# A hybrid decoder layer on one core: the first k group in seven products, LayerNorm's moments shifted, other orders for the pointwise and output products

## The chip, the core and the metric

The kernel runs on one core of a Trainium2 chip. Its time is the device time of one execution in microseconds (us); "the median" is that of several executions. A profiled execution also gives a trace: every instruction of each engine with its start and its duration. The engines are TensorE (PE, matrix products), VectorE (DVE), ScalarE (ACT), GpSimd (POOL) and SyncE (SP, which here only starts transfers). POOL too starts transfers, among them accumulating ones, which add their source to their destination.

## What is computed

The input x has 512 tokens of 2048 channels. The reference, cut to what matters:

```python
h = rms_norm(x, norm_g)
z = h @ w_in                                    # 2048 -> 7 x 1024
a_val, a_glu, a_gate, q, k, v, b_gate = split(z)
u = a_val * sigmoid(a_glu)                      # mixer A
u = causal_depthwise_conv(u, conv_w, conv_b)    # 31 taps
u = silu(layer_norm(u, conv_norm_g, conv_norm_b))
u = u @ conv_pw_w + conv_pw_b                   # 1024 -> 1024, "pointwise"
y_a = u * silu(a_gate)
q, k = rms_norm(q per head), rms_norm(k per head)   # mixer B, 16 heads of 64
o = dilated_attention_mixture(q, k, v)          # three windows
y_b = o * silu(b_gate)
out = x + concat(y_a, y_b) @ w_out              # 2048 -> 2048
```

## The kernel before

All large products are made channel by token, 128 channels by 512 tokens at a time, in PSUM tiles `ps_l`. Each f32 operand is split into a high and a low f16 part, and a product is three matmuls: high by high, high by low, low by high (`tri`, lines 414 to 416). Weights come in tiles `wf` of 4 x 128 rows by 512 columns (1 MB), through a ring of eight. For each tile ACT makes the high part (`split_hi`, `wh`) and DVE the low part (`split_lo`, `wl`), with a scale that is worked out from the sum of squares of the group's weights (`measure`, `bound`; each bound ends in a small sum on PE, a few steps on POOL, and `ws` and `wi` on DVE). Only the first two groups are made exactly, with f32 operands, line 895.

A **group** is 512 output columns of one part of `w_in` (`vg` value and GLU gate, `q`, `k`, `v`, `ag` and `bg` the two gates), of the pointwise weights (`pw`) or of `w_out` (`wb` and `wa`); a **unit** is one weight tile of it. The list `GROUPS` sets the order of units. A unit has eight **slots**: in each, PE makes six matmuls of 512 columns, and the other engines' work is written between the slots. Three mechanisms decide what is written where:

- `after(n, fn)` puts `fn` into a calendar n slots ahead, and `plan` lists do the same for the units in products of the kind below.
- `run_conv` writes a piece of the convolution (`cv`, DVE) whenever the DVE work written so far is behind a pace (`PACE`, ns per slot); LayerNorm is the tail of the same generator, `conv`.
- The engines run their own queues in order, each as soon as its waits are over. So an instruction that waits holds back everything behind it on its engine.

Groups in `SEVEN` are made with **seven products** instead of eight: the 2048 rows, the 512 columns and the tokens are halved, sums of weight blocks (`s1` to `s4`) and of x blocks (`tx`, from `xs`) are made, and 28 slots of twelve matmuls of 256 columns take the place of 32 slots. Their weights' sums are partly added by POOL's accumulating transfers (`wf<-wf`). The four output groups `wa` are always made so (`seven_parts`, `seven_products`), over `LENGTH` slots each. `w_out` has 16 row blocks, of 128 rows: rows 0 to 7 multiply mixer A's result y_a and 8 to 15 mixer B's, y_b, whose halves `b0` and `b1` have bounds of their own or share the one of y_a. `JOINED` names the output groups in which rows 8 to 11 (`b0`) are part of the seven products, with weights `wsd`; elsewhere they are plain units, `wb`.

LayerNorm before (lines 565 to 609): DVE adds the eight `cv` tiles into `lnacc`, PE sums over the channels (line 576), ACT makes `mean`, DVE subtracts it from each tile, ACT squares, DVE adds the squares into `lnacc2`, and `token_rsqrt` (line 391) sums these on PE with four small f32 products (line 395). Then each tile is scaled, passed through SiLU and split into `u16` for the pointwise product, which evacuates with a `tensor_scalar` and a multiplication by the gate.

Of the kernel before, what the change touches and what calls it, by code (L numbers as in the profile page):

```python
# [10 lines left out]
F32 = mybir.dt.float32  # L11
# [8 lines left out]
P = 128  # L20
S = 512
# [18 lines left out]
PACE = 1230  # L40
# [18 lines left out]
PACE_2 = 1480  # L59
MEASURE = 12  # L60
# [26 lines left out]
def layer(ctx: ExitStack, tc: tile.TileContext, xt, w1, w2, w3, g_in, conv_w, conv_b,  # L87
# [106 lines left out]
    def bound(name, sums, done, top=TOP):  # L194
# [7 lines left out]
        def sum_up():  # L202
            ps = s_ps.tile([P, S], F32, name="ps_s")
            T.matmul(ps[:, 0:n], ones16, sums, start=True, stop=True)
            V.tensor_reduce(scale, ps[:, 0:n], axis=AX.X, op=OP.add)
            G.tensor_scalar(scale, scale, 1e-30, 2.0 ** (-2 * top), op0=OP.max, op1=OP.mult)  # L206
            rsqrt(scale)
# [6 lines left out]
        after(2, sum_up)  # L214
        after(4, finish)
# [28 lines left out]
    for kind, g in GROUPS:  # L244
        if kind == "pw":
            units += [(w2, g, p, kind, g) for p in range(8 // KU)]
        elif kind in OUT_K:
            units += [(w3, g, p, kind, g) for p in OUT_K[kind] + (2,) * (kind == "wa" and g in JOINED)]
# [20 lines left out]
    def measure(i):  # L269
        if n_exact <= i < len(units):  # L270
            group = units[i][3:]
            mine = of_group[group]
# [6 lines left out]
            if not to_measure[group]:  # L279
                after(4, lambda: bound("w", sums.pop(group), lambda s, v: wscale.update({group: (s, v)}),  # L280
# [25 lines left out]
    def split_lo(i):  # L306
        if i < n_plain:
# [3 lines left out]
            after(11 if of_next(i) in SEVEN else 9, lambda: measure(i + RING))  # L311
# [79 lines left out]
    def token_rsqrt(acc, n, eps, c, row):  # L391

        pt = s_ps.tile([P, S], F32, name="ps_s")
        for t in range(NT):
            T.matmul(pt[:, 2 * t:2 * t + 2], acc[:, t * P:(t + 1) * P], ones[:, 0:2], start=True, stop=True)
        V.tensor_scalar(c, pt[:, 0:2 * NT].rearrange("p (t two) -> p t two", two=2)[:, :, 0], 1.0 / n, eps,
                        op0=OP.mult, op1=OP.add)
        rsqrt(c)
        yield
# [5 lines left out]
        yield  # L405
# [16 lines left out]
    def evac_scale(group):  # L422

        if group not in escale:
            other = {"pw": "u", "wa": "yab", "wb": "yb0"}.get(group[0])
# [83 lines left out]
    def evac_qk(half_i, t, ps, is_k):  # L509
# [9 lines left out]
        n = [2, 6 + 4 * t, 7 + 4 * t, 9 + 4 * t]  # L519
        if is_k and ("v", half_i) in SEVEN:  # L520
            n = [4 + 5 * (t > 0), 10 + 2 * t + 2 * (t > 0), 11 + 2 * t + 2 * (t > 0), 13 + 2 * t + 2 * (t > 0)]
# [22 lines left out]

    def conv():

        for i0 in range(0, 8, 2):
# [16 lines left out]
            elif i0 < 6:  # L564
                for i in (i0, i0 + 1):
                    V.tensor_add(acc, acc, cv[i])
                    yield 0

        wait[1] = True
        for i in (6, 7):  # L570
            V.tensor_add(acc, acc, cv[i])
        yield 3
        while any(0 <= clock[0] - n < 8 for n in at_pair.values()):
            yield 1
        mean = s_ps.tile([P, S], F32, name="ps_s")
        T.matmul(mean, ones, acc, start=True, stop=True)
        yield 1
        mean_sb = temp("mean")
        A.activation(mean_sb, mean, AF.Copy, scale=1.0 / C)
        acc = None  # L580
        yield 2
        acc2 = slot("lnacc2")
        squares = []
        for i in range(8):
            V.tensor_sub(cv[i], cv[i], mean_sb)
            if len(squares) > 1:
                V.tensor_add(acc2, acc2, squares.pop(0))
            if i == 0:
                A.activation(acc2, cv[i], AF.Square)
            else:  # L590
                squares.append(temp("lnsq"))
                A.activation(squares[-1], cv[i], AF.Square)
            yield 1 + i % 2
        while squares:
            yield 1
            V.tensor_add(acc2, acc2, squares.pop(0))
        yield 4
# [3 lines left out]
        row = temp("lnrow")  # L601
# [887 lines left out]
```

## Time and profile before

| what | value |
|---|---|
| median of 3 executions | 812.6 us (812.58 to 812.92) |
| the profiled execution | 812.95 us, span of its instructions 811.2 us |
| PE busy | 805.5 us (99%) |
| DVE busy | 707.2 us (87%) |
| ACT busy | 561.3 us (69%) |
| POOL busy | 136.2 us (17%) |
| PE's granted clock | full throughout |

In the rows quoted below, a row of a timeline has the start, the duration, the engine, the line and operation, the output and inputs by the program's names, the shape, and in brackets how long the engine was idle before and what it waited for. DVE's operations all have line 82 (a helper), so they are told apart by their tiles. Durations of instructions that follow each other closely overlap; the distance between two starts is what one costs. A row of windows has the stretch, its length, the busy time with the number of instructions, PE's clock, the share of the transfer engines and their GB/s. A row of transfers has the number, the size of each and the median time from issue to landing.

### The profile page before, as it was taken

How to read it: one execution, taken by the hardware profiler on the slowest of the kernel's cores; microseconds unless marked ns; L12 is line 12 of the kernel's file. 1: busy time of each engine (PE TensorE's matmuls, PEld its weight loads, DVE VectorE, ACT ScalarE, POOL GpSimd, SP SyncE). 2: the span in 40 equal slices, each digit the busy share in tenths (PEclk: the TensorE clock that was granted, in tenths of full speed). 3: DMA queues.
4: the chain of work that ended last, by engine and by line, in shares of the span. 5: the costliest groups of instructions: out<-in, count | busy, mean ns of one | idle time of the engine just before them, and what ended most of it. 6: DMA issues, size and time to landing. Idle time of an engine off the chain costs nothing.

```text
span 811.2 us, 13603 instructions
## 1 busy us (share of the span) xinstructions
PE 805.5 (99%) x5341; PEld 508.8 (63%) x5341; DVE 707.2 (87%) x1188; ACT 561.3 (69%) x788; POOL 136.2 (17%) x147
## 2 busy tenths in 40 slices
PE   9999999999999999999999999999999999999998
PEld 6888745888646854444444444444444447888887
DVE  6668999878989979999999989996689799979885
ACT  6667687577756688586756747587699968965541
POOL 0001021322223400004012010000100003432420
PEclk9999999999999999999999999999999999999999
DMA  9952345983875882526573634426352397898752
GB/s 337 355 212 91 117 93 144 136 255 57 308 150 108 121 296 94 128 104 169 143 182 102 164 112 125 118 88 165 104 120 102 110 278 165 170 249 198 131 103 68
DMA packets 100000, 127.19 MB, mean 157 GB/s; under 512 B 62560, under 2 KB 85344, under 8 KB 90720
## 3 DMA queue, kind: packets, MB, share of 16 engines
q1 hardware_dynamic: 80544, 107.37, 42.2%
q0 software_dynamic: 19104, 18.88, 16.3%
q8 instruction: 41, 0.67, 0.3%
q14 instruction: 23, 0.19, 0.1%
q10 hardware_dynamic: 288, 0.07, 0.0%
HBM read 88.56 MB, written 4.19 MB: 114 GB/s over the span
## 4 chain that ended last, share of the span: by engine, by line
PE 92%; DVE 4%; ACT 2%; DMA 1%; issue 1%; POOL 0%; ACTq 0%; DVEq 0%
PE ps_l L414 24%; PE ps_l L415 24%; PE ps_l L416 24%; PE ps_l L895 10%; PE ps_s L415 2%; PE ps_s L414 2%; PE ps_s L416 2%; PE ps_o L782 2%; PE ps_s L741 2%; DVE ws L82 1%; DMA pt<-hl 1%; DVE wl L82 1%; ACT junk L192 0%; DMA wf<-w_dram 0%; DVE cv L82 0%
## 5 line engine op out<-in xcount | busy, mean ns | idle before, releaser
L82 DVE SCALAR_TENSOR_TENSOR cv<-u,cw,cv 128x511 f32<-128x511 f32 (+14 forms) x240 | 162.0, 728 | 0.4 <-ACT cv L552 0.4
L192 ACT ACTIVATE junk<-wf 128x2048 uint8<-128x2048 f32 x68 | 129.2, 1900 | 9.4 <-DMA wf<-w_dram 9.0
L414 PE MATMUL ps_l<-x,wh 128*128 128x512 f16 x320 | 121.3, 379 | 0.4 <-DVE glu L82 0.4
L416 PE MATMUL ps_l<-x,wl 128*128 128x512 f16 x320 | 121.3, 379 | 0.0
L415 PE MATMUL ps_l<-x,wh 128*128 128x512 f16 x320 | 121.3, 379 | 0.0
L301 ACT ACTIVATE wh<-wf,ws 128x2048 f16<-128x2048 f32 x42 | 83.7, 1994 | 52.0 <-PE ps_l L415 50.2
L82 DVE SCALAR_TENSOR_TENSOR wl<-wf,ws,wh 128x2048 f16<-128x2048 f32 x43 | 100.9, 2346 | 12.1 <-ACT wh L301 12.1
L414 PE MATMUL ps_l<-wh,x 128*128 128x512 f16 x256 | 97.1, 379 | 0.0
L416 PE MATMUL ps_l<-wh,x 128*128 128x512 f16 x256 | 97.0, 379 | 0.0
L415 PE MATMUL ps_l<-wl,x 128*128 128x512 f16 x256 | 97.0, 379 | 0.0
L82 DVE SCALAR_TENSOR_TENSOR ws<-wf,ws 128x1024 f16<-128x1024 f32 x70 | 89.2, 1279 | 7.0 <-ACT ws L1173 4.5
L414 PEld LDWEIGHTS <-wh 128*128 128x128 f16 x448 | 43.9, 98 | 51.5 <-issue 4.0
L416 PEld LDWEIGHTS <-wl 128*128 128x128 f16 x448 | 43.8, 98 | 50.0 <-DVE wl L82 0.4
L415 PEld LDWEIGHTS <-wh 128*128 128x128 f16 x448 | 43.8, 98 | 47.1 <-issue 0.8
L895 PE MATMUL ps_l<-xr,wr 128*128 128x512 f32 x288 | 69.9, 398 | 0.1
L895 PEld LDWEIGHTS ps_l<-xr,wr 128*128 128x128 f32 x288 | 54.5, 190 | 13.7 <-ACT xr L339 1.0
L206 POOL TENSOR_SCALAR ws<-ws 128x1 f32<-128x1 f32 x20 | 9.4, 470 | 306.9 <-DVE ws L82 259.8
L414 PEld LDWEIGHTS <-x 128*128 128x128 f16 x352 | 34.4, 98 | 32.5 <-issue 1.9
L416 PEld LDWEIGHTS <-x 128*128 128x128 f16 x352 | 34.4, 98 | 31.3
L415 PEld LDWEIGHTS <-x 128*128 128x128 f16 x352 | 34.4, 98 | 30.1
L1173 ACT ACTIVATE ws<-wf,ws 128x1024 f16<-128x1024 f32 x42 | 47.1, 1138 | 5.7 <-PE ps_l L416 4.8
L170 POOL TENSOR_TENSOR ss<-ss,half 128x8 f32<-128x8 f32 x16 | 31.5, 1970 | 116.4 <-DVE ss L82 116.3
(265 smaller groups left out, 1871.3 us busy)
## 6 DMA issues: line engine op xcount, KB each, us to landing
wf<-w_dram SPq DMA_DIRECT2D x72, 1024.0 KB, 5.2
wf<-wf POOLq DMA_DIRECT2D x30, 512.0 KB, 6.3
x<-xt_dram SPq DMA_DIRECT2D x16, 256.0 KB, 6.6
res<-xt_dram SPq DMA_DIRECT2D x8, 512.0 KB, 6.7
out_dram<-res SPq DMA_DIRECT2D x15, 256.0 KB, 3.8
wf<-w_dram SPq DMA_DIRECT2D x7, 512.0 KB, 7.2
wf<-wf POOLq DMA_DIRECT2D x12, 256.0 KB, 5.8
wf<-w_dram SPq DMA_DIRECT2D x2, 256.0 KB, 3.4
```

Of the source, the lines that this page charges most:

```text
L82: return getattr(self.engine, name)(out, src, *args, **kw)
L170: G.tensor_tensor(ap, ap, half.to_broadcast(list(ap.shape)), op=OP.pow)
L192: A.activation(junk[:, :n], src, AF.Square, scale=scale, accum_out=acc)
L206: G.tensor_scalar(scale, scale, 1e-30, 2.0 ** (-2 * top), op0=OP.max, op1=OP.mult)
L301: A.activation(parts[i][0], raw[i], AF.Copy, scale=wscale[units[i][3:]][0])
L414: T.matmul(ps, ah, bh, start=first, stop=False, skip_group_check=more)
L415: T.matmul(ps, ah, bl, start=False, stop=False, skip_group_check=more)
L416: T.matmul(ps, al, bh, start=False, stop=last, skip_group_check=more)
L741: T.matmul(ps[i, a], qk["q", hf][p4 // 2][rows, p4 % 2, q, i * P:w], qk["k", hf][p4 // 2][rows, p4 % 2, k, :w], start=n == 0, stop=n == 2)
L782: T.matmul(po[rows, i * P:(i + 1) * P], vs[hf][j // 2][:, j % 2, 2 * p4 + a, vp * DH:(vp + 1) * DH], got["t", a][:, pp * (ALL // P) + FROM ...
L895: T.matmul(banks[group, m], wt[:, a, m * P:(m + 1) * P], xk[b], start=k == 0 and a == b == 0, stop=k == KC - 1 and a == 1)
L1173: A.activation(t[:, 0], block(name, pair), AF.Copy, scale=wscale[group][0])
```

## The change

1. The first k group joins `SEVEN`, with tables (`IN_ADD`, `IN_HI`, `IN_OUT`, `NORM_7`) for the slots of its steps, and the x sums run from slot 60 in steps of 9 (before 58 and 10).
2. LayerNorm: after six tiles PE sums them, and ACT makes the mean of these six as a shift (`shifted`). It is subtracted from all tiles, and six are squared while the convolution of the last pair runs. Five of the additions of squares, and two of the additions of `cv`, are accumulating transfers of POOL. The last two tiles are squared when the convolution ends; their sum `lnlast` (that of all tiles is nil but for these two, after the shift) gives the rest of the mean, and the variance is the mean of squares less its square (`less` in `token_rsqrt`).
3. The order of groups: `pw` comes one unit later (behind `wb` 0), both `pw` groups share one scale, and the evacuation is one operation, with the bias scaled ahead (`pw_bias`).
4. `JOINED` becomes (1, 2): output group 0 has rows 8 to 11 (`wb` 0) and rows 12 to 15 (a new unit `wc`) as plain units, its seven products take 14 slots, and `b1` gets a bound and scale of its own.
5. Slots: the low half of a weight one slot later (`SPLIT_AT`), `measure` and `bound` at other slots, a pace of seven steps instead of two, and tables for the `wa` groups (`WA_PARTS`, `WA_ADD`, `WA_OUT`).

```diff
-PACE = 1230
+PACE_FROM = (65, 117, 171, 227, 299, 363)
+PACE = [1170, 1350, 1300, 1295, 1480, 1465, 1480]
...
-          ("ag", 0), ("ag", 1), ("bg", 1), ("pw", 0), ("pw", 1)]
-JOINED = (0, 1)
-GROUPS += [("wb", g) for g in range(4) if g not in JOINED] + [("wa", g) for g in range(4)]
-OUT_K = {"wb": (2,), "wa": (3, 0, 1)}
-
-SEVEN = (("vg", 3), ("q", 0), ("v", 0))
+          ("ag", 0), ("ag", 1), ("bg", 1), ("wb", 0), ("pw", 0), ("pw", 1), ("wb", 3), ("wc", 0)]
+JOINED = (1, 2)
+GROUPS += [("wa", g) for g in range(4)]
+OUT_K = {"wb": (2,), "wc": (3,), "wa": (3, 0, 1)}
+
+SEVEN = (("vg", 3), ("q", 0), ("k", 0), ("v", 0))
-SUM_FROM = 58
-SUM_STEP = 10
+SUM_FROM = 60
+SUM_STEP = 9
+SPLIT_AT = [0, 3]
...
 def token_rsqrt(acc, n, eps, c, row, less=None):
...
+            for n_sum, a in enumerate((acc,) if less is None else (acc, less)):
+                at = 2 * (NT * n_sum + t)
+                T.matmul(pt[:, at:at + 2], a[:, t * P:(t + 1) * P], ones[:, 0:2], start=True, stop=True)
...
+    def square(i):
+        V.tensor_sub(cv[i], cv[i], shift[0])
+        if not acc2:
+            acc2.append(temp("lnacc2"))
+            A.activation(acc2[0], cv[i], AF.Square)
+        else:
+            squares.append(temp("lnsq"))
+            A.activation(squares[-1], cv[i], AF.Square)
+
+    def shifted():
+        ps = s_ps.tile([P, S], F32, name="ps_s")
+        T.matmul(ps, ones, shift[0], start=True, stop=True)
+        A.activation(shift[0], ps, AF.Copy, scale=1.0 / (6 * P))
+        yield
+        for i in range(6):
+            square(i)
+            yield
+            if squares:
+                yield
+                nc.gpsimd.dma_start(acc2[0], squares.pop(0), accum_op=OP.add)
...
         for i in (6, 7):
-            V.tensor_add(acc, acc, cv[i])
...
+            square(i)
+        last2 = temp("lnlast")
+        V.tensor_add(last2, cv[6], cv[7])
+        yield LN_STEPS[1]
+        for _ in range(2):
+            V.tensor_add(acc2[0], acc2[0], squares.pop(0))
...
+        mean_ps = s_ps.tile([P, S], F32, name="ps_s")
+        T.matmul(mean_ps, ones, last2, start=True, stop=True)
...
         elif kind == "pw":
-            t = temp("ya")
-            V.tensor_scalar(t, ps, evac_scale(group), pwb[:, i:i + 1], op0=OP.mult, op1=OP.add)
             y = ag.pop(i)
-            def gate():
-                V.tensor_mul(y, y, t)
-                put_y("a", i, y)
-            after(1, gate)
+            V.scalar_tensor_tensor(y, ps, pwb[:, i:i + 1], y, op0=OP.add, op1=OP.mult)
+            put_y("a", i, y)
...
-    LENGTH = [29, 28, 21, 21]
+    LENGTH = [14, 28, 28, 21]
...
-            adds = [(-8, "s3", add), (-2, "s2", add), (3, "s1", add), (4, "s4", add),
...
-            begin = {"a11": -6, "a11d": -4, "a22": -3, "a22d": 4, "a12": 0, "s1": 6, "a12d": 11, "s3": 12, "s1d": 14, "s2": 15,
-                     "s3d": 18, "s4": 20, "s2d": 21, "s4d": 24}
+WA_ADD = [{'s1': (4,), 's4': (1,), 's2': (-2,), 's3': (-8,)}, ...
+WA_PARTS = [{'a11': (-29,), 'a22': (-27,), 'a12': (-1,), 's3': (1,), 's2': (4,), 's1': (7,), 's4': (9,)}, ...
...
-                extra[0].append(lambda: split_hi(i + 1))
-                extra[2].append(lambda: split_lo(i + 1))
+                extra[SPLIT_AT[0]].append(lambda: split_hi(i + 1))
+                extra[SPLIT_AT[1]].append(lambda: split_lo(i + 1))
```

In the two `WA` rows (shown for output group 0) the numbers are slots from the group's start: `WA_ADD` says when a sum of weights is formed, `WA_PARTS` when ACT makes its high part; DVE makes the low part one slot later. Before, `adds` and `begin` said the same.

The order of instructions shows where three of these land. First DVE in the third `vg` group, between the evacuation of a first product (`u`, `glu`) and the low half `wl` of the second unit's weights. `xn` is a normalised x tile, `x_…` its low part. Before:

```order
L82 SCALAR_TENSOR_TENSOR xn<-x,gs,rrow 128x512
L82 TENSOR_TENSOR xs<-xn 128x256 x2
L82 SCALAR_TENSOR_TENSOR xs<-xs,xn 128x256 x2
L82 TENSOR_TENSOR glu<-ps_l,rrow 128x512
L82 TENSOR_TENSOR u<-ps_l,rrow 128x512
L82 TENSOR_TENSOR u<-u,glu 128x512
L82 TENSOR_TENSOR x_940<-xn,x_940 128x512
L82 SCALAR_TENSOR_TENSOR xn<-x,gs,rrow 128x512
L82 TENSOR_TENSOR tx<-xs,tx 128x2x256 x2
L82 TENSOR_TENSOR x_967<-xn,x_967 128x512
L82 SCALAR_TENSOR_TENSOR wl<-wf,ws,wh 128x2048
```

The same place in the changed kernel:

```order
L103 SCALAR_TENSOR_TENSOR xn<-x,gs,rrow 128x512
L103 TENSOR_TENSOR glu<-ps_l,rrow 128x512
L103 TENSOR_TENSOR u<-ps_l,rrow 128x512
L103 TENSOR_TENSOR u<-u,glu 128x512
L103 TENSOR_TENSOR xs<-xn 128x256 x2
L103 SCALAR_TENSOR_TENSOR xs<-xs,xn 128x256 x2
L103 TENSOR_TENSOR x_936<-xn,x_936 128x512
L103 SCALAR_TENSOR_TENSOR xn<-x,gs,rrow 128x512
L103 TENSOR_TENSOR x_967<-xn,x_967 128x512
L103 TENSOR_TENSOR tx<-xs,tx 128x2x256 x2
L103 SCALAR_TENSOR_TENSOR xn<-x,gs,rrow 128x512
L103 SCALAR_TENSOR_TENSOR wl<-wf,ws,wh 128x2048
```

The four `xs` operations stand behind the second `glu` instead of ahead of it, and one `xn` more stands ahead of `wl`.

Second, the end of the convolution: DVE before, from the last `cv` subtractions on,

```order
L82 TENSOR_TENSOR cv<-cv,mean 128x512
L82 TENSOR_TENSOR lnacc_5516<-lnacc_5516,lnsq 128x512
L82 TENSOR_REDUCE ws<-ps_s 128x1
L82 ISA sx,st_5720<-ps_s,tab 128x512
L82 ISA st_5720 128x1
L82 ISA sx,st_5721<-ps_s,tab 128x512
L82 ISA st_5721 128x1
L82 SCALAR_TENSOR_TENSOR wl<-wf,ws,wh 128x2048
```

and in the changed kernel DVE, where `sx` is the evacuation of attention scores,

```order
L103 SCALAR_TENSOR_TENSOR cv<-u,cw,cv 128x482
L103 TENSOR_TENSOR cv<-cv,lnacc 128x512 x3
L103 TENSOR_TENSOR lnlast<-cv 128x512
L103 ISA sx,st_5902<-ps_s,tab 128x512
L103 ISA st_5902 128x1
L103 ISA sx,st_5903<-ps_s,tab 128x512
L103 ISA st_5903 128x1
L103 TENSOR_TENSOR lnacc_5241<-lnacc_5241,lnsq 128x512 x2
L103 SCALAR_TENSOR_TENSOR wl<-wf,ws,wh 128x2048
```

and POOL, up to its part of LayerNorm's reciprocal root (`lncol`):

```order
L601 DMA lnacc_5241<-lnsq 128x512
L227 TENSOR_SCALAR ws<-ws 128x1
L191 TENSOR_TENSOR ws<-ws,half 128x1
L227 TENSOR_SCALAR ws<-ws 128x1
L191 TENSOR_TENSOR ws<-ws,half 128x1
L601 DMA lnacc_5241<-lnsq 128x512 x2
L459 TENSOR_TENSOR esc<-wi,xinv 128x1
L601 DMA lnacc_5241<-lnsq 128x512 x2
L227 TENSOR_SCALAR ws<-ws 128x1
L191 TENSOR_TENSOR ws<-ws,half 128x1
L191 TENSOR_TENSOR lncol<-lncol,half 128x4
```

The additions of squares between the subtractions are gone from DVE, `lnlast` is new, and five transfers stand in POOL's queue; `lnlast` waits for the last of them, since it takes its source's buffer.

Third, POOL at the output groups, before,

```order
L427 TENSOR_TENSOR esc<-wi,yabi 128x1
L1026 TENSOR_SCALAR nesc<-esc 128x1
L1030 TENSOR_TENSOR wjs<-ws,yabs 128x1
L1031 TENSOR_TENSOR wjs<-wjs,yb0i 128x1
L955 DMA wf<-wf 128x4x256
L955 DMA wf<-wf 128x2x256
L955 DMA wf<-wf 128x4x256
```

and in the changed kernel:

```order
L459 TENSOR_TENSOR esc<-wi,yb1i 128x1
L1034 DMA wf<-wf 128x4x256 x4
L1034 DMA wf<-wf 128x2x256 x2
L459 TENSOR_TENSOR esc<-wi,yabi 128x1
L1085 TENSOR_SCALAR nesc<-esc 128x1
L1089 TENSOR_TENSOR wjs<-ws,yabs 128x1
L1090 TENSOR_TENSOR wjs<-wjs,yb1i 128x1
```

Six additions for groups 0 and 1 stand together ahead of the scales of the next group.

More of the change, by code (lines that the diff above doesn't have):

```diff
@@ L567, in conv @@
                     yield 0
+            if i0 == 4:
+                shift.append(acc)
+                steps = shifted()
+                for n in range(40):
+                    after(SHIFT_FROM + n * SHIFT_STEP, lambda: next(steps, None))
         wait[1] = True
+        yield LN_STEPS[0]
+        for _ in steps:
+            pass
         for i in (6, 7):
-            V.tensor_add(acc, acc, cv[i])
[L572 to L597, printed above, removed]
+            square(i)
[4 more added lines that the diff above has]
+            V.tensor_add(acc2[0], acc2[0], squares.pop(0))
+        yield LN_STEPS[2]
         while any(0 <= clock[0] - n < 8 for n in at_pair.values()):
@@ L869, in run_conv @@
     def run_conv():
[L871 removed]
+        pace = PACE[sum(clock[0] >= n for n in PACE_FROM)]
         V.load = min(max(V.load - pace, -pace), 4 * pace)
```

317 lines of the change are left out of this document (170 added, 147 removed).

## The prediction

> **What bounds the kernel now.** I read the page first: busy times, then the chain that ended last. After them came the list of what TensorE (PE) waits for, then single rows of PE and VectorE (DVE) at the places the change touches. PE is busy in 805.5 of 811.2 us and carries 92% of the chain; DVE is next with 87%, so it has some 100 us of air, but not everywhere.
>
> ```profile
> span 811.2 us, 13603 instructions
> PE 805.5 (99%) x5341; PEld 508.8 (63%) x5341; DVE 707.2 (87%) x1188; ACT 561.3 (69%) x788; POOL 136.2 (17%) x147
> PE 92%; DVE 4%; ACT 2%; DMA 1%; issue 1%; POOL 0%; ACTq 0%; DVEq 0%
> PE ps_l L414 <- DVE glu L82: 0.4, 1, 0.4
> PE ps_s L741 <- DVE st L82: 0.3, 1, 0.3
> PE ps_l L415 <- DVE ws L82: 0.2, 1, 0.2
> PE ps_o L782 <- DMA pt<-hl: 0.2, 1, 0.2
> ```
>
> In the last four rows the columns are total, times and longest wait: after the start, PE hardly waits. So the time is PE's content plus very little. A gain must come out of PE's content, and every new lateness of DVE or of a transfer that exceeds its slack is paid in full.
>
> **PE's content, step by step.** A matmul's own duration (0.38 us) overlaps the next one, so the price is the distance between starts.
>
> ```profile
> 171.89 0.27 PE L414 MATMUL ps_l<-x,ws 128*128 128x256 f16 x1
> ...
> 172.98 0.27 PE L415 MATMUL ps_l<-x,ws 128*128 128x256 f16 x1
> 542.77 1.02 PE L576 MATMUL ps_s<-lnacc,ones 128*128 128x512 f32 x2
> 543.63 0.38 PE L414 MATMUL ps_l<-x,wh 128*128 128x512 f16 x1
> ...
> 544.28 0.38 PE L414 MATMUL ps_l<-x,wh 128*128 128x512 f16 x1
> 578.61 0.95 PE L395 MATMUL ps_s<-ones,lnacc 128*128 128x2 f32 x8
> 579.42 0.38 PE L414 MATMUL ps_l<-x,wh 128*128 128x512 f16 x1
> ```
>
> Ten starts lie between the first two rows: 0.109 us for 256 columns. Three lie between 543.63 and 544.28: 0.217 us for 512. The f32 column sum (L576, one matmul in the program) holds PE for 0.86 us, and the four small f32 products of the LayerNorm column (L395, x8 in the trace) for 0.81 us.
>
> - First k group in seven products: 192 matmuls of 512 columns (four units of eight slots of six) become 336 of 256 (28 slots of twelve): 41.7 becomes 36.6, −5.1 us.
> - Rows 12 to 15 plain for output group 0, and `JOINED` moved from groups 0 and 1 to 1 and 2: 48 matmuls of 512 come, 96 of 256 go: +10.4 − 10.5, −0.1 us.
> - LayerNorm: a second f32 column sum (one for the shift, one for the mean of what is left), +0.86. `token_rsqrt` now also takes `lnlast`: four more small products, +0.81.
> - One more bound (`yb1`): one small sum on PE, about a tenth of the 0.81, +0.1.
>
> Sum: −3.4 us. Nothing hides this term, because PE is the bound; if no wait grew, the run would end near 812.6 − 3.4 = 809.2 us.
>
> **Place A, the first f16 units (86 to 122 us).** The sums `xs` and `tx` for the seven products start two slots later (`SUM_FROM` 58 to 60), and the low half of a weight (`split_lo`) is asked for one slot later.
>
> ```profile
> 96.42 0.40 PE L895 MATMUL ps_l<-xr,wr 128*128 128x512 f32 x1
> 97.20 0.38 PE L414 MATMUL ps_l<-x,wh 128*128 128x512 f16 x1 [0.38 <-DVE glu L82]
> 107.77 0.38 PE L415 MATMUL ps_l<-x,wh 128*128 128x512 f16 x1
> 108.10 0.39 PE L416 MATMUL ps_l<-x,wl 128*128 128x512 f16 x1
> 86.52:108.04 21.52, 21.18 (x33) 1.00 0.29 98
> 103.23 0.74 DVE L82 SCALAR_TENSOR_TENSOR xn<-x,gs,rrow 128x512 f32<-128x512 f32 x1
> 103.90 1.29 DVE L82 TENSOR_TENSOR tx<-xs,tx 128x512 f16<-128x512 f32 x2
> ...
> 105.70 2.34 DVE L82 SCALAR_TENSOR_TENSOR wl<-wf,ws,wh 128x2048 f16<-128x2048 f32 x1
> ...
> 116.99 0.15 DVE L82 TENSOR_SCALAR ws<-ws 128x1 int32<-128x1 int32 x1
> 117.17 0.16 DVE L82 RECIPROCAL wi<-ws 128x1 f32<-128x1 f32 x1
> ```
>
> DVE is busy in 21.18 of 21.52 us here (the window row: length, busy, instructions), and PE waits for it twice: about 0.5 us for `glu`, and 0.12 us for the second `wl` (108.10 comes 0.33 after 107.77, not 0.22). DVE is the bound of this place, so what is put ahead of that `wl` is paid. The order of the changed kernel has one `xn` more ahead of it (0.67 us between starts), and the pair `ws`, `wi` of a scale (0.15 to 0.25). That is +0.8 to +0.9 us; I take +0.9. The ends are 0 (the pair and the `xn` find a gap) and 1.5 (the third `wl`, which also gets work ahead of it, runs out of its slack).
>
> **Place D, the end of the convolution (about 551 to 567 us).** Before, all sums of LayerNorm were additions on DVE. Now five squares go through accumulating DMAs issued by GpSimd (POOL) into `lnacc2`, each waiting for the one before. The addition `lnlast` on DVE reuses the buffer of the last square, so it waits for the last DMA to land. Queued behind it on DVE stand two score evacuations, two `lnacc` additions and a `wl`.
>
> ```profile
> wf<-wf POOLq DMA_DIRECT2D x12, 256.0 KB, 5.8
> 567.12 0.69 DVE L82 CUSTOM_DVE_ANT_0 sx<-ps_s,tab 128x512 f32<-128x512 f32 x1 [3.67 <-PE ps_s L741]
> 568.35 2.35 DVE L82 SCALAR_TENSOR_TENSOR wl<-wf,ws,wh 128x2048 f16<-128x2048 f32 x1
> 570.61 0.69 DVE L82 TENSOR_TENSOR lnacc<-lnacc,lnsq 128x512 f32<-128x512 f32 x1
> DMA  9999979999994999400000000000000000948997
> ```
>
> Counting the program's work slot by slot, the fifth square is ready near 555 us: ACT does it behind a `gate` evacuation that waits for PE. With 5.8 us to land (the nearest row: the same kind and size) `lnlast` starts near 561. Then come 0.6 + 2 × 0.6 + 2 × 0.6 + 2.26 = 5.3 us, so `wl` is done near 566.3, and PE wants it near 566.5. It just fits or just fails; the second batch of scores also needs the banks that the first two `sx` free, near 563. The DMA engines are idle in the middle of this stretch (the last row shows 550 to 575 us in 40 slices), which favours a landing that isn't slower than 5.8. I take +0.3, ends 0 and 2.
>
> Here the Trainium skill speaks, in "DMA: Bandwidth & Descriptors" (section on the anatomy of one SWDGE DMA): such a DMA takes about 2.0 us plus its bytes over 436 GB/s, which by an estimate from that formula is 2.6 us for 256 KB. By it D would cost nothing and the sum would be 0.3 us lower. The trace's 5.8 disagrees, and I go by the trace.
>
> **Place C, output groups (672 to 710 us).** `wa0` now lasts 14 slots instead of 29. A seven slot is 12 × 0.109 = 1.31 us.
>
> ```profile
> 680.00:700.00 20.00, 19.69 (x33) 1.00 0.56 86
> 690.00:710.00 20.00, 20.00 (x30) 1.00 0.82 171
> wf<-wf POOLq DMA_DIRECT2D x3, 512.0 KB, 5.7
> wf<-wf POOLq DMA_DIRECT2D x3, 256.0 KB, 14.6
> wf<-wf POOLq DMA_DIRECT2D x1, 512.0 KB, 12.3
> ```
>
> The two windows show DVE full before the change, with PE not waiting. The DMA rows are those issued in 669 to 690 us (the first) and in 696 to 702 (the other two). The sums of weights that POOL adds by DMA used to have 20, 17 and 16 slots from the addition to the first use by ACT; the new tables give `s3` 9, `s2` 6 and `s4` 8, the shortest being 7.9 us. Against the 5.7 of the nearest place that holds; against the 12.3 of four in a row it doesn't. DVE has the splits of `wa0` and `wa1` closer together, and `y<-gate,yb1s` for `wc0` ahead of them, which by my count is about 0.15 us late. I take +0.5 for both; ends 0 and 5.
>
> **Stalls that go.**
>
> ```profile
> 625.54 0.38 PE L414 MATMUL ps_l<-u,wh 128*128 128x512 f16 x1
> 625.97 0.38 PE L415 MATMUL ps_l<-u,wh 128*128 128x512 f16 x1
> ```
>
> The pointwise product now starts behind a `wb` unit, 8 × 1.3 = 10.4 us later against LayerNorm, so this wait for `u` (0.43 − 0.22 = 0.21) should go: −0.2. Its cover is that unit; if LayerNorm ends over 10 us later than before, the wait is back. The other moves I cost at nothing: the seven products of k put about 33 us of DVE work beside 36.6 us of PE. `pw`'s evacuation loses a step on DVE and gains none on PE. The accumulating DMAs of `lnacc` have a whole convolution pair to land.
>
> **Sum.** −3.4 + 0.9 + 0.3 + 0.5 − 0.2 = −1.9 us. The profiled run took 812.95 us (span 811.2 and 1.75 around it), so this makes 811.05; the median, 812.6, is 0.35 lower, so 810.7 us. Least: −3.4 and all four named waits gone (0.5 + 0.12 + 0.2 + 0.2), 808.2. Most: +1.5 + 2 + 5 − 3.4, 817.7.
>
> **Rivals.** About 0.2% (1.6 us) is what a measurement can tell from no change: faster is below 811.0, slower above 814.2.
>
> 1. The saving comes whole: A finds a gap, D and C fit their slack. 812.6 − 3.4 − 0.2 = 809.0; with half of A, 809.5. For it: PE waits nowhere else before. Against: DVE's 21.18 of 21.52.
> 2. DVE eats it: A 1.5, D 1.5, C 1.0, also 0.3 at the start of k's products, as before at `ws` (0.2 in the list). 812.6 − 3.4 + 4.3 − 0.2 = 813.3; with half of the extras about 812. For it: the full windows. Against: k's products have slack by count.
> 3. Slower: the landing of `s2` in `wa0`. ACT waits for it from 7.9 us after its issue; the product needs it ten slots after the issue, 13.1 us, less 1.1 for ACT's half and 1.2 for DVE's, so 10.8. Landing in 14.6, as in the last group of rows, would hold PE for 3.8 us: 810.7 + 3.8 = 814.5. It decides from a landing of 14.3 us on. Against: only one stretch of the trace shows such landings, where four were issued together.
>
> A rule of the Trainium skill bears on rival 3: "SBUF — State Buffer", section "Who interferes with whom", says that POOL, while DVE runs a copy or a tensor_scalar in a two-port mode, can't write the descriptors of its DMAs. No row here separates this from a plain queue behind other transfers.
>
> **Chances.** Forecast (810.0 to 811.5) 0.40, rival 1 (809.9 or less) 0.24, rival 2 (811.6 to 814) 0.25, rival 3 0.11. Faster: rival 1 and about two thirds of the forecast, 0.52; same 0.36; slower 0.12. The range reaches from rival 1 to the top of rival 2: 808.9 to 813.8.
>
> **What the changed profile would show.** PE: 336 matmuls of 256 columns where k had 192 of 512, 28 slots in 36.6 us. A: `glu` wait near 0.6, the gap ahead of the first product with the second `wl` near 0.8 instead of 0.12. D: DVE idle for 5 to 8 us ahead of `lnlast`, put down to a DMA, and PE's wait behind it under 1 us. C: DVE's windows at 20 of 20, PE's waits for `ws` or `wsd` under 1 us together, no wait of ACT for a POOL DMA over 2 us. 626: no gap. The prediction is wrong if PE's waits together exceed 3.5 us, or if A's gaps are gone.

## The result, and the profile after

The changed kernel takes 832.1 us (median of six executions, 827.6 to 834.8) against 812.7 for the one before on the same chip: ratio 1.023, 95% interval 1.020 to 1.026. The prediction said 810.7 with a range of 808.9 to 813.8, so it was wrong in sign and by 21 us. The profiled execution took 830.74 us, 17.8 more than the 812.95 of before. First the page of the changed kernel: span, busy times, PE's granted clock in 40 slices, and the chain that ended last by engine.

```profile
span 829.0 us, 13900 instructions
PE 807.0 (97%) x5448; PEld 520.1 (63%) x5448; DVE 716.6 (86%) x1203; ACT 572.0 (69%) x800; POOL 174.1 (21%) x170
PEclk9999999999999899999999999999999999999999
PE 73%; DVE 13%; DMA 7%; POOL 3%; issue 2%; ACT 2%; SPq 0%; DVEq 0%; POOLq 0%; ACTq 0%
```

PE carried 92% of the chain before and carries 73% now; transfers rose from 1% to 7%. PE's count agrees with the prediction's: +144 for k, −48 for rows 8 to 15, +2 and +8 (the two f32 sums as the trace counts them), +1 for the bound, together +107, which is 5448 − 5341. So the content was saved as worked out, and the time was lost in waits. The list of PE's waits (total, times, longest):

```profile
PE ps_l L447 <- DVE ws L103: 9.9, 3, 5.5
PE ps_o L861 <- DMA pt<-hl: 2.8, 2, 1.7
PE ps_s L225 <- ACT junk L213: 1.6, 1, 1.6
PE ps_l L447 <- DVE y L103: 1.0, 2, 0.8
PE ps_s L448 <- DVE ws L103: 0.7, 1, 0.7
PE ps_l L446 <- DVE glu L103: 0.6, 1, 0.6
PE ps_l L448 <- DVE wl L103: 0.6, 1, 0.6
PE ps_l L448 <- DVE wsd L103: 0.4, 1, 0.4
```

The first row is new and the largest: PE stands (it waits with nothing to do) for weights `ws` of the seven products of k and v. The windows of the stretch from 215 to 290 us, of the kernel before and then of the changed one, show it whole (length, busy PE, PEld, DVE, ACT, POOL with counts, PE's clock, share of the transfer engines, GB/s):

```profile
215.00:290.00 75.00, 75.00 (x514) 49.86 (x513) 67.15 (x91) 47.03 (x52) 24.55 (x19) 1.00 0.72 148
```

```profile
215.00:290.00 75.00, 64.90 (x563) 56.26 (x562) 59.00 (x77) 49.68 (x58) 32.56 (x25) 0.93 0.99 179
```

Before, PE is busy for 75.00 of 75. In the changed kernel 10.1 us are missing, and the mean clock of 0.93 says that part of the rest ran slower as well. DVE is busy for 59 of 75 us: it isn't full, it waits. What it waits for is in the chain (start, length, what):

```profile
200.56 0.84 POOL wf L1208
201.40 19.45 DMA wf<-wf
...
221.50 0.04 POOL wf L1208
...
222.33 2.19 POOL ss L191
...
245.84 19.85 DMA wf<-wf
...
267.18 2.20 POOL ss L191
269.40 0.69 DVE cb L103
...
271.44 1.29 DVE ws L103
```

Read from the top: POOL issues the two additions for k's `s1` at 200.6. The second lands 19.5 us later. Only then does POOL issue the addition for `s2` (221.5), which takes the sum as a source, and behind it in POOL's queue stands the reciprocal root of the head norm (`ss`, 222.3), which doesn't need that sum at all. DVE needs `ss`, and the low half `ws`, for which PE stands, is queued behind that on DVE. The timelines of DVE and PE show the last two steps of k's case:

```profile
224.56 0.69 DVE L103 TENSOR_TENSOR cb<-cb,ss 128x512 f32<-128x512 f32 x1 [6.13 <-POOL ss L191]
226.59 1.28 DVE L103 SCALAR_TENSOR_TENSOR ws<-wf,ws 128x1024 f16<-128x1024 f32 x1
227.93 0.27 PE L447 MATMUL ps_l<-ws,tx 128*128 128x256 f16 x1 [4.11 <-DVE ws L103]
228.80 0.42 PE L446 MATMUL ps_l<-ws,tx 128*128 128x256 f16 x1
229.02 0.42 PE L447 MATMUL ps_l<-ws,tx 128*128 128x256 f16 x1
...
231.55 0.27 PE L447 MATMUL ps_l<-ws,tx 128*128 128x256 f16 x1
231.66 0.27 PE L448 MATMUL ps_l<-ws,tx 128*128 128x256 f16 x1
```

After the stand PE runs slower for a while: from 228.80 to 229.02 is 0.22 us where the same matmul takes 0.11 (231.55 to 231.66). Sixteen of them at +0.105 are 1.7 us more. The same comes again for v at 272.8, behind a stand of 5.7 us. The stretch in sum, by distances between PE's starts: stands of 4.27, 0.44, 0.37 and 5.67, and 3.2 for the two slow runs, 14.0 us.

Of the 17.8 us lost these 14 are the main part. The rest, again by distances between starts: attention's transposed `pt` +2.6, the output groups +4.4 (`ysum`, whose sum PE makes for the bound of y, 1.78; `y` 0.96; `ws` 0.81; `wsd` 0.53; `wsc` 0.33), place A +0.8, against −3.4 of content and −0.2 at 626. Together that is +18.2.

### The profile page after: what moved, and what is told of

Same layout as the page of the kernel before. It is cut to its first block, busy times and chain, and to the rows that moved or that the text cites. A ratio compares the mean times of both kernels' runs of the same rounds, so it can differ in the third digit from the quotient of the medians.

```text
span 829.0 us, 13900 instructions
## 1 busy us (share of the span) xinstructions
PE 807.0 (97%) x5448; PEld 520.1 (63%) x5448; DVE 716.6 (86%) x1203; ACT 572.0 (69%) x800; POOL 174.1 (21%) x170
## 4 chain that ended last, share of the span: by engine, by line
PE 73%; DVE 13%; DMA 7%; POOL 3%; issue 2%; ACT 2%; SPq 0%; DVEq 0%; POOLq 0%; ACTq 0%
PE ps_l L446 18%; PE ps_l L447 18%; PE ps_l L448 18%; PE ps_l L974 10%; DMA wf<-wf 5%; DVE cv L103 2%; PE ps_s L448 2%; PE ps_s L447 2%; PE ps_s L446 2%; DVE wl L103 2%; PE ps_s L820 2%; DVE ws L103 2%; PE ps_o L861 2%; POOL ss L191 1%; DVE res L103 1%
## 5 line engine op out<-in xcount | busy, mean ns | idle before, releaser
L103 DVE SCALAR_TENSOR_TENSOR ws<-wf,ws 128x1024 f16<-128x1024 f32 x84 | 107.2, 1280 | 7.1 <-ACT ws L1212 5.3
L326 ACT ACTIVATE wh<-wf,ws 128x2048 f16<-128x2048 f32 x39 | 77.7, 1992 | 30.3 <-PE ps_l L447 25.1
L103 DVE SCALAR_TENSOR_TENSOR wl<-wf,ws,wh 128x2048 f16<-128x2048 f32 x39 | 91.5, 2346 | 3.3 <-ACT wh L326 3.3
L446 PEld LDWEIGHTS <-wh 128*128 128x128 f16 x432 | 42.3, 98 | 54.0 <-issue 5.0
L447 PEld LDWEIGHTS <-wh 128*128 128x128 f16 x432 | 42.2, 98 | 49.0 <-issue 1.0
L446 PE MATMUL ps_l<-wh,x 128*128 128x512 f16 x192 | 72.9, 380 | 0.0
L448 PE MATMUL ps_l<-wh,x 128*128 128x512 f16 x192 | 72.8, 379 | 0.0
L447 PE MATMUL ps_l<-wl,x 128*128 128x512 f16 x192 | 72.8, 379 | 0.0
L1212 ACT ACTIVATE ws<-wf,ws 128x1024 f16<-128x1024 f32 x56 | 62.3, 1136 | 10.1 <-DMA wf<-wf 6.6
L447 PE MATMUL ps_l<-ws,tx 128*128 128x256 f16 x192 | 53.8, 280 | 9.9 <-DVE ws L103 9.9
L227 POOL TENSOR_SCALAR ws<-ws 128x1 f32<-128x1 f32 x20 | 18.2, 910 | 202.6 <-DVE ws L103 202.2
L446 PE MATMUL ps_l<-ws,tx 128*128 128x256 f16 x192 | 53.8, 280 | 0.2 <-ACT ws L1212 0.2
L448 PE MATMUL ps_l<-ws,tx 128*128 128x256 f16 x192 | 53.9, 281 | 0.0
```

Of the source, the lines that this page charges most:

```text
L103: return getattr(self.engine, name)(out, src, *args, **kw)
L227: G.tensor_scalar(scale, scale, 1e-24 if name == "u" else 1e-30, 2.0 ** (-2 * top), op0=OP.max, op1=OP.mult)
L326: A.activation(parts[i][0], raw[i], AF.Copy, scale=wscale[units[i][3:]][0])
L446: T.matmul(ps, ah, bh, start=first, stop=False, skip_group_check=more)
L447: T.matmul(ps, ah, bl, start=False, stop=False, skip_group_check=more)
L448: T.matmul(ps, al, bh, start=False, stop=last, skip_group_check=more)
```

## Which part of the change brings the loss

Two theories stood against each other at first. One: a queue, in which POOL's late additions hold the head norm and so DVE and PE. The other: k's seven products give DVE more than it can do beside PE. The first three experiments take one piece away each. In each diff the left side is the changed kernel, if nothing else is said.

**k plain again.**

```diff
-SEVEN = (("vg", 3), ("q", 0), ("k", 0), ("v", 0))
+SEVEN = (("vg", 3), ("q", 0), ("v", 0))
```

> The changed kernel with the first k group in eight products again (its 192 matmuls of 512 columns back, +5 us of PE), all else of the change kept. If the loss of 14 us in 215 to 285 us comes from two groups in seven products next to each other: those waits go, 832.1 + 5 - 14 = 823. If it comes from other tables of the change (the sums one to three slots later, weights one slot later): waits of that size stay, 837.

Measured: 828.6 us (827.9 to 829.8), ratio 1.019 [1.017, 1.021]; neither number. The stretch from 215 to 290 is whole again (under 0.2 us lost), so k's seven products do bring the 14 us. But PE then stands at LayerNorm instead:

```profile
PE ps_l L448 <- DVE wl L103: 3.5, 2, 2.9
PE ps_s L652 <- DVE lnlast L103: 1.6, 1, 1.6
```

Distances between starts give 5.9 us lost from 540 to 560 and 4.4 from 597 to 603, some of it at the slow clock behind a stand. So the change's tables and paces don't suit a program without k's products.

**The kernel before, with only k added to the seven products.**

```diff
-SEVEN = (("vg", 3), ("q", 0), ("v", 0))
+SEVEN = (("vg", 3), ("q", 0), ("k", 0), ("v", 0))
```

> The kernel before with one edit: the first k group in seven products (PE -5 us), the old tables otherwise. Its POOL queue has the same order of s1, ss, s2 as the changed kernel. Queue theory: the same waits, 10 to 16 us with the half clock: 812.7 - 5 + 13 = 818 to 824. If the loss comes from the other tables of the change: 808.

Measured: 833.0 us (832.4 to 835.5), ratio 1.025 [1.024, 1.027], again outside. Only 4.3 us go at 220 to 280, and 16 at LayerNorm:

```profile
PE ps_s L395 <- DVE lnacc L82: 3.7, 1, 3.7
PE ps_l L414 <- ACT u L316: 3.6, 1, 3.6
```

PE has 5 us less to do ahead of LayerNorm and waits there for DVE's sums and for `u`. The other parts of the change (shifted moments, `pw` one unit later) cover this: in the run with `s1` on DVE below, where k's products cost PE nothing, its list has 0.5 us of waits at LayerNorm. The 4.3 us also say that k's products needn't cost 14; what differs is read below.

**The s1 sums of k and v on DVE.**

```diff
-                nc.gpsimd.dma_start(block(to, pair), block(x, pair), accum_op=OP.add)
+                if name == "s1" and kind in ("k", "v"):
+                    V.tensor_tensor(block(to, pair), block(to, pair), block(x, pair), op=OP.add)
+                else:
+                    nc.gpsimd.dma_start(block(to, pair), block(x, pair), accum_op=OP.add)
```

> The changed kernel with the s1 sums of the k and v groups added by DVE (two operations of 1.2 us a group) instead of by POOL's transfers; the order of the rest stays. Queue theory: s2 no longer waits for a slow landing of s1, ss passes, the two long waits go: 818 to 822. Late-weights theory: the same. Full-DVE theory: 4.9 us more work on DVE in these stretches, so 834 to 838.

Measured: 815.1 us (814.2 to 816.7), ratio 1.003 [1.002, 1.004]: better than any of the theories allowed. An addition in DVE's timeline, the window as above, and DVE's wait for the head norm's root:

```profile
206.37 1.22 DVE L103 TENSOR_TENSOR wf<-wf 128x1024 f32<-128x1024 f32 x1
```

```profile
215.00:290.00 75.00, 75.00 (x690) 65.54 (x689) 69.97 (x102) 60.56 (x70) 29.84 (x23) 1.00 0.92 204
```

```profile
DVE cb L103 <- POOL ss L191: 0.7, 2, 0.4
```

Four additions of 1.22 us, so 4.9 us more work on DVE, and PE is busy for 75 of 75 us at full clock. DVE, given more, is busy for 70 us where it was for 59. So the theory that DVE has no room falls, and 17 of the 19 us hang on these four transfers (the attention's 2.6 us went with them). Whether it is their lateness, the next section shows.

## Why the additions land late

In the changed kernel k's pair takes 13.1 and 19.5 us from issue to landing, and v's 9.5 and 19.9; in q's group, 26 us before k's, the same pair takes 7.2 and 7.5. The four rows are transfers of POOL in the changed kernel (those issued at 199 to 204 us, and at 174 to 177), in the kernel before with k added (197 to 200), and in the one before (235 to 250, v's pair): number, size, median landing. A median of two hides that the second of a pair lands later: the last two rows are 5.8 and 9.3, and 5.7 and 8.7.

```profile
wf<-wf POOLq DMA_DIRECT2D x2, 512.0 KB, 16.3
```

```profile
wf<-wf POOLq DMA_DIRECT2D x2, 512.0 KB, 7.4
```

```profile
wf<-wf POOLq DMA_DIRECT2D x2, 512.0 KB, 7.5
```

```profile
wf<-wf POOLq DMA_DIRECT2D x2, 512.0 KB, 7.2
```

The candidate is in SP's queue: when the blocks of q come free, SP issues four weight loads of 1 MB between 201.8 and 208.0, right on top of k's pair. These loads are not new: in the kernel before four go out from 203.0 to 207.6, but no addition stands near them, since k was plain. With only k added to the kernel before, the pair went out at 198.0 and the first load at 205.4. Theory 1 says that the loads make the additions late; theory 2, that POOL's transfers are late there by themselves.

**The additions of s2 behind the head norms**, to see whether freeing POOL's queue is enough.

```diff
-IN_HI = [-5, -5, -5, -5, -5, -5, -4]
-IN_ADD = {..., ('s2', 0): -1, ('s2', 1): 0, ...
+IN_HI = [-5, -5, -5, -3, -5, -5, -4]
+IN_ADD = {..., ('s2', 0): 4, ('s2', 1): 5, ...
```

> The changed kernel with one table entry moved: the two s2 additions of each seven-product input group are asked for at slots 4 and 5 instead of -1 and 0 (their high parts two slots later), so that in POOL's queue the roots ss of the head norms stand ahead of them. Queue theory (POOL waits at s2 for the landing of s1, 13 to 19 us; ss behind it holds DVE, DVE holds the weights' low part, PE stands 4.3 and 5.7 us and then runs at half clock): the two long waits go, PE's wait for ws falls from 9.9 us to under 2, time 818 to 822. Late-weights theory (the sums themselves land too late for PE): the order in the queue doesn't matter, waits of 4 to 6 us stay, 829 to 833. Full-DVE theory (DVE has more work than these 36 us hold): 829 to 833.

Measured: 840.6 us (837.3 to 842.0), ratio 1.034 [1.031, 1.036]; worse, and no theory had that. The head norm is no longer held, but the landings of `s1` stay at 13.3 and 20.0, and the delay goes to DVE, whose own sum `s3` overwrites what `s2` reads:

```profile
DVE wf L103 <- DMA wf<-wf: 9.8, 2, 7.7
```

Reordering POOL's queue doesn't help while the landing is late: the next queue that needs the data is held in its turn.

**Measuring the weights three slots sooner.**

```diff
-MEASURE = 16
+MEASURE = 13
```

> The changed kernel with one number changed: the weights that a seven-product group fetches are measured 13 slots later instead of 16, so that their scale ws passes POOL some 3 us earlier, and the s1 additions of k and v, which stand behind it in POOL's queue, are issued ahead of the four weight loads instead of among them. Collision theory (the additions land in 13 to 19 us because four loads of 1 MB are issued in the same microseconds): landing 6 to 10 us, PE's loss in 215 to 290 us falls from 14 to 5 or less, 821 to 824. Port theory (POOL's descriptors are held up by DVE's work): landing stays 13 to 19 us, 830 to 834.

Measured: 842.7 us (839.9 to 845.1), ratio 1.038 [1.035, 1.041]. The additions don't go out sooner (202.1), but the first load goes out 4 us later (205.9). The landings do fall, to 6.9 and 12.8, but this moves ACT's work too: it now waits for the very loads, as its row says, and PE waits for ACT.

```profile
216.32 1.91 ACT L213 ACTIVATE junk<-wf 128x2048 uint8<-128x2048 f32 x1 [8.63 <-DMA wf<-w_dram]
```

```profile
PE ps_l L447 <- DVE ws L103: 9.0, 9, 2.3
PE ps_l L446 <- ACT ws L1212: 7.7, 2, 4.1
```

Too much moved at once for the time to be a verdict on the landing.

**The loads ahead of the transposing transfers in SP's queue**, and **the loads written six slots later**.

```diff
+TURN = 12
...
-                        turn_qk(store[x], 2 * z + m, src[:, 2 * m:2 * m + 2])
+                        after(TURN, lambda m=m: turn_qk(store[x], 2 * z + m, src[:, 2 * m:2 * m + 2]))
```

> The changed kernel with one edit: the transposing transfers of q's and k's seven products are written twelve slots later, so that in SP's queue the four weight loads of 1 MB stand ahead of them and are issued as their buffers come free (about 191 to 202 us), not in one burst at 201.8 behind a wait for qhl. POOL's additions, DVE's and ACT's work are as in the changed kernel. Theory 1 (the additions for s1 land late because they share the transfer engines with the burst of loads): the landings of the two s1 additions near 200 us fall from 13.1 and 19.5 us to 7 to 11, PE's long waits at 228 us shrink to under 1.5 us and the time falls by 3 to 8 us, to 824 to 829 (v0 keeps part of its burst). Theory 2 (they land late for a reason of POOL's own, whatever else is in flight): landings of 13 and 19 us as before, 831 to 834.

```diff
+LATE = 6
...
-                    load(i0 + j + RING)
+                    after(LATE, lambda j=j: load(i0 + j + RING))
```

> The changed kernel with one edit: each 1 MB weight load that takes the place of a seven-product group's block is written six slots (7.9 us) later, so in the program it stands at about 208 to 216 us instead of 202 to 208; nothing of POOL, DVE or ACT is moved, so the two s1 additions near 200 us are issued as before but with no weight load in flight. Theory 1 (they land late because they share the transfer engines with these loads): they land in 6 to 10 us instead of 13.1 and 19.5, and the POOL queue's hold at 221 us is gone; ACT measures the weights soon after and may now wait some us for the later loads, so the time is open, 820 to 836. Theory 2 (POOL's accumulating transfers land late by themselves there): 13 and 19 us again.

Measured: 829.4 us (828.3 to 831.6) and 832.4 (825.8 to 834.1). Both edits failed to do what they say. In the first the loads go out at 200.4, 202.2, 206.3 and 208.1, in the second at 201.8, 202.8, 206.1 and 207.9, nearly as in the changed kernel, and the landings are the old ones (13.8 and 19.4 in the first, and the second's row):

```profile
wf<-wf POOLq DMA_DIRECT2D x2, 512.0 KB, 16.2
```

SP has little else in its queue. In both runs its waits ahead of these loads are for DVE's `ws`, the step that reads the buffer last. So a load goes out as soon as its buffer comes free, even where it is written six slots (7.9 us) later. So neither tells the theories apart; that 829.4 lies in theory 1's band proves nothing. To move a transfer it must stand in the queue of an engine that is itself on time.

**The loads in ACT's queue, seven slots later; and, as control, in ACT's queue at once.**

```diff
-                    load(i0 + j + RING)
+                    after(7, lambda j=j: load(i0 + j + RING, queue=nc.scalar))
```

> The changed kernel, but the four weight loads of 1 MB that follow each group in seven products are issued by ACT instead of SP and stand seven slots later in its queue, which by ACT's rows is 208 us for the first and about 215 us for the other three, instead of 202 to 208. POOL's additions are not touched. Theory 1 (the s1 additions land late because they share the transfer engines with these loads): the pair of 200 us lands in 5.5 to 10 us instead of 13.1 and 19.5, and the additions of s2, issued near 214, take the collision in their place, with landings over 8 us. ACT then measures the weights soon after the loads and may wait for them, so the time says little: 822 to 838. Theory 2 (POOL's transfers are late by themselves there): 13 and 19 us again.

> The control for the later loads: the same loads issued by ACT, but not later in the program. Theory 1: issued at 202 to 208 as before, landings of s1 13 and 19 us within 2 us. Theory 2: the same. If the landings fall here too, the issuing queue matters and not the time of the loads.

Measured: 822.6 us (820.7 to 825.0), ratio 1.012 [1.010, 1.015], for the later loads; 833.1 for the control (one execution). The later loads, rows of ACT's queue, then POOL's transfers issued at 174 to 176, at 199 to 204 and at 212 to 222 us, then the window as above:

```profile
202.94 0.33 ACTq L288 DMA_DIRECT2D wf<-w_dram  x1
211.85 1.30 ACTq L288 DMA_DIRECT2D wf<-w_dram  x3
```

```profile
wf<-wf POOLq DMA_DIRECT2D x2, 512.0 KB, 14.4
...
wf<-wf POOLq DMA_DIRECT2D x2, 512.0 KB, 10.8
...
wf<-wf POOLq DMA_DIRECT2D x2, 512.0 KB, 11.2
```

```profile
215.00:290.00 75.00, 71.70 (x658) 62.37 (x656) 66.84 (x88) 56.82 (x66) 33.56 (x25) 1.00 1.01 213
```

and the control's pair:

```profile
wf<-wf POOLq DMA_DIRECT2D x2, 512.0 KB, 17.0
```

Three of the four loads now go out 9 us behind the pair, and the pair lands in 9.5 and 12.0 us instead of 13.1 and 19.5; the three meet the additions of `s2` instead, which take 11.2 where they took 6.4. In the control, with the loads at 201.9 to 211.7, it is 14.7 and 19.3. In the run with later loads, the pair of q, which landed in 7.4 us in the changed kernel, now has three loads beside it and takes 14.4. The additions follow the loads, not POOL. Theory 1 is shown, and 9.5 of the 19.4 us came back by the loads' time; the control says that the change of queue by itself brings nothing. The stretch from 215 to 290 us, where the changed kernel lost 14.0 us by distances between starts, loses 4.8.

## What is left beside the landing

From the kernel with `s1` on DVE I tried to take out the remaining waits, each by a slot number.

**Two places**: the low half one slot earlier everywhere, with the x sums and the y bound's steps moved.

```diff
-SUM_FROM = 60
-SUM_STEP = 9
+SUM_FROM = 58
+SUM_STEP = 10
...
-YB = [0, 2, 4, -2, -2, 2]
+YB = [0, 2, 4, -2, 2, 4]
...
-SPLIT_AT = [0, 3]
+SPLIT_AT = [0, 2]
```

> The changed kernel with the s1 sums of k and v on DVE (as in the run before, 815.1), and two more edits: the slots of the x sums and of the low half of a weight as before the change (place A), and the bound of all y summed two slots later (PE stood 1.6 us for its squares near 684). If A's loss is the order of xn and ws on DVE ahead of the second wl: PE's gaps there fall from 1.46 to 0.66. If the wait for the squares is only one of placing: it goes. Both: 815.1 - 0.8 - 1.6 = 812.7; if what is moved comes late elsewhere: 814 to 816.

Measured: 821.0 us (819.4 to 822.9), ratio 1.011 [1.009, 1.012]. Both waits shrink (at A from 1.5 to 0.9 us, `ysum` from 1.78 to 0.45), and others appear in the attention, perhaps since the convolution's pieces come at other slots (not shown):

```profile
PE ps_s L820 <- DVE gate L103: 2.2, 1, 2.2
PE ps_s L225 <- DVE st L103: 2.1, 1, 2.1
```

**Four places, and the three late ones of them.** Both have `YB`'s last two at 1 and 3, the scales of output group 1 written in slot 1 of group 0 instead of slot 4, and one more step in LayerNorm (`LN_STEPS` 2 to 3); the first also has the low half one slot earlier in the second and third `vg` group.

> The changed kernel with the s1 sums of k and v on DVE (815.1 when alone), and four small moves: the low half of a weight one slot earlier again, for the third and fourth vg groups only; the bound of all y summed three slots later; the scales of output group 1 three slots earlier, ahead of four transfers in POOL's queue; LayerNorm's sums on PE one slot later. If each wait is what it seems (0.7 at the second wl, 1.3 of 1.8 at the squares, 1 at LayerNorm, some 0.5 to 1 at the weights of output group 1): 815.1 - 3.5 = 811.6 to 812.5. If what is moved comes late elsewhere, as in the kernel with the x sums moved back (821): 814 to 820.

> As the kernel sent with it, but without the move in the vg groups, so that everything up to LayerNorm stays as in the 815.1 us kernel. If the waits are what they seem: 815.1 - 2.8 = 812.3. If the move in the vg groups is what upsets the attention groups (the convolution's pieces shift against them): this one is the faster of the two by more than 1 us.

Measured: 818.1 us (817.9 to 820.4), ratio 1.008 [1.006, 1.009], and 813.9 (812.8 to 815.6), ratio 1.0017 [1.0008, 1.0026]. The edit at A, early in the kernel, costs 4 us in the attention and LayerNorm; the three late ones gain 1.2.

**The y bound's steps two slots later still; then also the low half of one weight earlier; then LayerNorm one step more.** Here the left side is the kernel with three late places, and each edit comes on top of the last.

```diff
-YB = [0, 2, 4, -2, 1, 3]
+YB = [0, 2, 4, -2, 3, 5]
...
-                extra[SPLIT_AT[1]].append(lambda: split_lo(i + 1))
+                extra[SPLIT_AT[1] - (i == of_group["vg", 2][0])].append(lambda: split_lo(i + 1))
...
-LN_STEPS = [4, 1, 3, 2, 4, 4, 1, 1]
+LN_STEPS = [4, 1, 4, 2, 4, 4, 1, 1]
```

> As the experiment with three late places mended (813.9), but the two steps that sum all of y's squares for its bound stand two slots later in the table (3, 5 instead of 1, 3), so that ACT's square of the last y has been written ahead of PE's small sum. Theory A (each of PE's remaining waits is a slot number too tight by 1 to 2 us and can be mended by itself): PE's 1.77 us wait for junk goes, 812.2 to 813.0. Theory B (what is moved later there only makes the scale late for the next group's weights): the wait turns up again at ws or wsd, 813.6 to 815.

> As the one with the bound's steps two slots later, and the low half of one weight only, that of the second f16 unit of the third value and gate group, is written one slot earlier. Theory A: the 0.72 us gap at 109 us goes too, 811.5 to 812.4. Theory B: since DVE is full there, the convolution pieces come at other slots and stalls appear at LayerNorm and the attention, as when two units got this edit; 813.5 to 818.

> As the one with the bound's steps later and the low half earlier, and LayerNorm's third step count is 4 instead of 3, so that PE's column sum of lnlast is written one slot later. Theory A: the waits of 0.30 and 0.64 us near 560 us go as well, 810.8 to 811.6. Theory B: LayerNorm's end is then late for the pointwise product, 814 to 818.

Measured: 815.6 us (815.2 to 817.5), 820.5 (818.6 to 822.0) and 823.1 (818.8 to 823.4); ratios 1.004, 1.009 and 1.011. Theory A falls each time, but all three medians lie above theory B's ranges too. B's mechanism shows in the first, where PE's wait for `junk` goes and comes back as `y` and `ws`:

```profile
PE ps_l L447 <- DVE y L103: 1.9, 2, 1.7
PE ps_s L448 <- DVE ws L103: 0.9, 1, 0.9
```

It shows in the second as well: waits for `pt` (1.6 us), `st` and `lnacc` (1.0 each) stand in PE's list. In the third, PE doesn't wait for `u`, so LayerNorm isn't late for the pointwise product as B had it, and the cause of that run's time stays open.

No version beat the kernel before. The best is 0.17% behind it.

## Why the prediction was wrong

- **PE's content, −3.4 us: right**, by the count of matmuls above. With `s1` on DVE, where PE's waits are down to some 7 us against 1.5 before, the span is 1.6 us above that of before, which leaves about −3.8 for the content.
- **The failed step: "The other moves I cost at nothing: the seven products of k put about 33 us of DVE work beside 36.6 us of PE."** It measured +14 us. The sum of DVE's work was not wrong (DVE took 4.9 us more there without loss). What it left out are the transfers and the queue: that k's additions fall among the four loads that follow the release of q's blocks (203.0 to 207.6 us in the trace of before), so that they land in 13.1 and 19.5 us, and that the head norm's root stands behind the next addition in POOL's queue. I had costed the k group's content and its DVE work, but followed none of its transfers, though the trace of before had a landing of 14.6 us beside other transfers, quoted for place C.
- **Rival 3 was the right mechanism at the wrong place.** A landing of POOL's additions did decide the sign, for `s1` of k and v, not for `s2` of `wa0`: ACT waited for no landing in `wa0`. Later in the output groups it waited up to 5.2 us for one (at 747 us), over the 2 us that the prediction allowed, but PE didn't stand behind it.
- **Place A, +0.9: right**, measured +0.8 (`glu` 0.73 and the second `wl` 0.73 by distances between starts, before 0.55 and 0.12).
- **Place D, +0.3: within its ends of 0 and 2.** DVE waits for the last square, longer than the 5 to 8 us foreseen. PE doesn't wait for it in the changed kernel, to which it comes late by the loss ahead; with `s1` on DVE the two sums behind it (`lnlast`, `lnacc`) come about 0.9 us late. The row is of the changed kernel:

```profile
DVE lnlast L103 <- DMA lnacc<-lnsq: 9.4, 1, 9.4
```

- **Place C, +0.5: mis-sized, though within its end of 5.** It measured 4.4: 2.6 for `y`, `ws`, `wsd` and `wsc`, and 1.8 at the bound of y, whose square on ACT is queued behind a gate; that wait was not foreseen at all. DVE's window at 680 to 700 us, with the bound of y, holds 18.2 of 20 us, so there it isn't full; the one at 690 to 710, with the first wait for `y`, holds 19.9.
- **626, −0.2: right**, no gap there. The attention's +2.6 for `pt` was not foreseen; it is gone with `s1` on DVE, but 3.7 us stand in the list of the run with later loads, so its cause stays open.
- The prediction's own test, PE's waits together above 3.5 us, is what failed: the list holds over 17.

## What to carry to other kernels

Before a faster form of a product is costed by its matmuls and by each engine's total work, write down for its stage every transfer that it issues and every buffer that it frees, with the times: what lands late holds an in-order queue, and the cost is paid by the unrelated instruction behind it. An accumulating transfer on the path is cheap only while nothing large is in flight; where an engine has a few microseconds of room, the addition belongs there. And a transfer written later in an idle queue isn't issued later: check in the trace that an edit moved what it was to move.

## What the hardware showed

- In the changed kernel a POOL addition of 512 KB with no load issued beside it lands in 5.6 to 7.1 us (issued at 182 to 185 and 221 to 224 us). With four loads of 1 MB issued within 8 us of the pair, the first lands in 13.1 and 9.5 us and the second in 19.5 and 19.9 (k's and v's pair). The Trainium skill, "DMA: Bandwidth & Descriptors" (anatomy of one SWDGE DMA), gives by its formula an estimate of 3.2 us for that size; no landing here is that short.
- PE runs at half its clock after a stand: 0.21 us instead of 0.11 per matmul of 256 columns for some 3.4 us after a stand of 4.3, 1.7 us more. So a wait of 4 us costs nearly 6. The window of the changed kernel from 228.2 to 231.3 has the granted clock, the third number from the end:

```profile
228.20:231.30 3.10, 3.10 (x16) 2.23 (x15) 2.15 (x4) 2.60 (x5) 2.50 (x2) 0.50 1.19 160
```

This agrees with the Trainium skill, "TensorE: Matmul & The Clock Gate" (Part 1, the HAM clock gate), by which an idle window of about 3.4 us brings half rate and a busy one of the same length ends it. But with k plain a shorter stand, of 3.1 us, brought half the clock too (0.50 from 600.4 to 602.9), so the length isn't a safe limit; the stand of 1.8 us at the bound of y in the changed kernel did not (1.00 from 684.2 to 686.0).
